# A hybrid decoder block in float32: a list scheduler in the kernel fixes the order of each engine's instructions

## The chip, the cores and the metric

One core of one Trainium2 chip. The metric is device microseconds of one execution of the whole block; lower is better. The kernel before takes 1054.05 us (median of 3 runs, 1053.57 to 1054.77). The engines of the core are called PE (matmuls; PEld is its loading of weights), DVE (VectorE), ACT (ScalarE), POOL (GpSimd) and SP (the queue that issues all the transfers here). Each takes its own instructions strictly in the order in which the compiled program has them, and an instruction that waits holds back all those behind it on its engine.

## The reference

One block over 1024 tokens of width 1024, all float32. A vector c gives shift, scale and gate columns; the rest is two sub-layers with residuals and a last norm:

```python
cond = silu(c) @ ada_w + ada_b
shift1, scale1, gate1, shift2, scale2, gate2 = split(cond, 6)
h = rmsnorm(x, norm1_g) * (1 + scale1) + shift1
u, v, val, gate = split(h @ w_in + b_in, 4)          # 512 columns each
y_a = spatial_gating_mixer(gelu(u), gelu(v), ...)    # layernorm of v, causal 128x128 mix in chunks of 128 tokens
y_b = conformer_conv_mixer(val, gate, ...)           # val * sigmoid(gate), causal depthwise conv of width 31, group norm, silu
y = concat(rmsnorm(y_a), rmsnorm(y_b))
x = x + gate1 * (y @ w_out)
h2 = rmsnorm(x, norm2_g) * (1 + scale2) + shift2
g_ff, up_ff = split(h2 @ w_ffn_in, 2)                # 2 x 2816 columns
x = x + gate2 * ((silu(g_ff) * up_ff) @ w_ffn_out)
out = rmsnorm(x, norm_f_g) * (1 + scale_f) + shift_f
```

## The kernel before, in words

Everything is kept transposed: 128 features on the partitions, tokens along the free dimension, in two halves of 512 tokens. A float32 matmul is made of three fast ones: weights and activations are split into a high part (an ACT copy in the reduced type) and a low part (a subtraction on DVE or POOL), and `mm3` (lines 185 to 189) and `product` (505 to 511) run high x high, low x high and high x low.

**First phase (before about 75 us).** The conditioning columns are dot products: `ada_cols` (133 to 144) loads a 128x1024 tile and DVE multiplies it by silu(c) and sums along the rows (line 143). For each of eight slices of h the shift and the scale column are made, then the slice (`modulated`, 197 to 213), and PE accumulates it into eight PSUM banks of the projections val and gate.

**Mixers.** `u_proj`, `v_proj`, `vg_proj` are the projections of each half of the tokens; `conv_pair` is the convolution, tap by tap on DVE (line 448), for the first half partly on ACT and POOL; `spatial` is the causal mix; `branch_out` the norms; `w_out` the projection back, with the residual into `xs`. During the up-projection x itself lies in HBM (`x_mid`) and its SBUF tiles serve as buffers.

**FFN.** The up-projection uses a 2x2 fast product with seven multiplications over halves of tokens and pairs of tiles: `stationary` (591 to 623) loads the weights of a tile, forms their sums and differences (lines 611 to 617) and splits them (`split`, 501 to 503); `run` accumulates the seven products, and lines 729 to 755 combine them. For 20 of the 22 tiles two of the products, which need the first half of the tokens alone, are made before, while the second half is still in the mixers (`ahead_quad`, 518 to 528, its matmuls at line 510 with the output ah), and put away in HBM. The results go to HBM (line 662) and come back for the down-projection in three rounds, of the same form, which adds into `xs` at line 859. The last 24 conditioning columns (gate2, shift_f, scale_f) are loaded into two tiles of x that are free meanwhile (`last_columns`, 683 to 685, queued by lines 687 to 689) and multiplied by line 143. The last norm and the outputs (lines 807 to 829) close the kernel.

**Buffers.** Tiles with the same tag share a fixed number of slots: three PSUM banks for the tag mm, two each for cv and gn, one for nrm; four slots for raw weights (raw), eight for split ones (w), and so on. A new tile waits for a slot to come free. The pool `ffn` uses the memory of the pools `mid` and `front` again, once these are closed.

**The order.** The framework traces the program, finds the dependences through tiles, and then its own scheduler, which simulates a time line with durations of its own, sets each engine's order: by the program's order as priority, with some work raised (`tc.high_priority`, around the norms) or held back by hand. Four such holds exist, each `with tc.issue_after(ins)`, which lets an engine take what stands in the block only after `ins` on the same engine: the matmuls of `vg_proj(1, (3,), r2_ready, 12)` from the thirteenth slice on (its last 12 matmuls) behind the last matmul of the norm `n2_0` (lines 326 to 328); the loads of the second half of x, of the u weights and of the mixer's operands behind the load of the first phase's last column (line 532); the change of the ACT's table behind the last silu (line 762); and the tail behind an instruction of the down-projection (line 900).

Of the kernel before, what the change touches and what calls it, by code (L numbers as in the profile page):

```python
# [1 line left out]

# [11 lines left out]
P = 128  # L14
# [38 lines left out]
def tile_order():  # L53

    n = N_AHEAD + N_FILL
    whole = {round(i * (NF - 1) / (NF - n - 1)): n + i for i in range(NF - n)}
    begun = iter(range(n))
    return [whole[i] if i in whole else next(begun) for i in range(NF)]


@with_exitstack
def block_kernel(ctx: ExitStack, tc: tile.TileContext, xT, c, ada, cols, vbias, bs, wsp,
                 wv, wu, wvg, wo, wf, wfo, wfl, cst, out):
    nc = tc.nc
    V, A, G, PE = nc.vector, nc.scalar, nc.gpsimd, nc.tensor

    const = ctx.enter_context(tc.tile_pool(name="const", bufs=1))
    sb = ctx.enter_context(tc.tile_pool(name="sb", bufs=1))
# [31 lines left out]
    def hs(half):  # L100
        return slice(half * H, (half + 1) * H)
# [31 lines left out]
    def ada_cols(i, n=1, pool=False, dst=None):  # L133
        for j in range(i, i + n):
            raw = dst
            if raw is None:
                raw = sb.tile([P, D], F32, tag="raw", name=f"ada{j}", bufs=N_RAW)
            ada_dma[j] = nc.sync.dma_start(raw, ada[j])
# [4 lines left out]
            V.scalar_tensor_tensor(raw, raw, 1.0, cact, op0=ALU.mult, op1=ALU.mult,  # L143
                                   accum_out=cond[:, j:j + 1])

    def ccol(m, k, n=1):
        return cond[:, m * 8 + k:m * 8 + k + n]
# [27 lines left out]
    last = {}  # L175
# [139 lines left out]
    first_phase_loaded = ada_dma[SCALE1 * 8 + KD - 1].ins  # L315
# [213 lines left out]


    background += [lambda i=i: ada_cols(GATE1 * 8 + i) for i in range(8)]
    with tc.issue_after(first_phase_loaded):
        for k in range(KD):
            nc.sync.dma_start(xs[k][:, hs(1)], xT[k, :, hs(1)])
        u_proj(0)
        load_mixer_operands()
# [43 lines left out]
    ffn = ctx.enter_context(tc.tile_pool(name="ffn", bufs=1, reuse_waits="tile"))  # L580
# [7 lines left out]
    def ev(name):  # L588
        return ffn.tile([P, H], F32, tag="ev", name=name, bufs=N_EV)
# [35 lines left out]
    for f in range(N_AHEAD, N_AHEAD + N_FILL):  # L625
        t = ffn.tile([P, 2, H], F32, tag="m3", name=f"ahead_{f}", bufs=4)
# [67 lines left out]
    order = tile_order()  # L694
# [118 lines left out]
    def output(i, tiles=range(KD), by_pool=()):  # L813
        bank, part = norm_banks[i], pieces[i]
        size = part.stop - part.start
        if by_pool:
            r = ev(f"r_nf{i}")[:, 0:size]
            A.activation(r, bank[:, 0:size], AF.Copy)
        for k in tiles:
            t = ev(f"of{i}_{k}")[:, 0:size]  # L820
            if k in by_pool:
                G.tensor_tensor(t, xs[k][:, part], r, op=ALU.mult)
                A.activation(t, t, AF.Identity, bias=ccol(SHIFTF, k), scale=ccol(SCALEF, k))
                nc.sync.dma_start(out[k, :, part], t)
                continue
            V.scalar_tensor_tensor(t, xs[k][:, part], ccol(SCALEF, k), bank[:, 0:size],
                                   op0=ALU.mult, op1=ALU.mult)
            A.activation(t, t, AF.Identity, bias=ccol(SHIFTF, k))
            nc.sync.dma_start(out[k, :, part], t)
# [3 lines left out]
    f0 = 0  # L833
    for r, pairs in enumerate(ROUNDS):
        last_round = r == len(ROUNDS) - 1
        mov = [{} for _ in range(pairs)]
        for m in (1, 5, 6, 2, 7, 4, 3):
            for p in range(pairs):
                t = ev(f"a{r}_{p}_{m}")
# [5 lines left out]
        base = 0 if last_round else 8 * r  # L845
# [36 lines left out]
        for n, m in ((0, 1), (0, 5), (0, 6), (0, 2), (0, 7), (1, 1), (0, 4), (0, 3), (1, 6), (1, 2), (1, 7),  # L882
# [4 lines left out]
            last_ins = step(n, m)  # L887
# [29 lines left out]
    output(0, (3, 5, 6, 7), by_pool=(3, 5))  # L917
    output(1)
    output(2)


# [73 lines left out]
```

## Time and profile before

| what | value |
|---|---|
| time, median of 3 runs | 1054.05 us (1053.57 to 1054.77) |
| the profiled execution's own time | 1055.96 us |
| its span, first to last instruction | 1053.9 us |
| granted PE clock, mean over the span | 0.976 |
| PE busy | 983.6 us (93%) |
| DVE busy | 868.5 us (82%) |
| ACT busy | 466.4 us (44%) |
| POOL busy | 413.2 us (39%) |
| moved through HBM | 183 MB, 174 GB/s over the span |

In the profile's lines, times are microseconds from the start of the span. A stretch's row gives its length and, for each engine, the busy time in it with the count of its instructions. A group's row gives line, engine, operation, output<-inputs, shape and count, then the busy time and the mean duration in ns, then the idle time just before these instructions with what ended it. In the chain of work that ended last, each piece stands with its start and duration. "issue" is time in which the engine waited for nothing that the profile shows.

### The profile page before, as it was taken

Reading aid. Unit: us, or ns where it says so; the run is one execution under the profiler, and the core shown is the slowest. Engines: PE = TensorE matmul, PEld = TensorE weight load, DVE = VectorE, ACT = ScalarE, POOL = GpSimd, SP = SyncE. Lnnn points to the kernel's source line nnn. Section 1 sums busy time; section 2 is a strip of 40 time slices with the busy share of each in tenths; the row PEclk is TensorE's granted clock in tenths of the full one; section 3 lists DMA queues with packets and bytes.
Section 4 is the critical chain, followed back from the end, with each engine's and each line's share of the span. In section 5 each row is a group of like instructions: output and inputs, shape, how many; then the busy total and the mean of one; then the engine's idle time right before and its main releaser. Section 6 shows DMA issues by size and latency. Waiting matters only on the chain.

```text
span 1053.9 us, 13171 instructions
## 1 busy us (share of the span) xinstructions
PE 983.6 (93%) x4613; PEld 783.7 (74%) x4613; DVE 868.5 (82%) x1216; ACT 466.4 (44%) x732; POOL 413.2 (39%) x240
## 2 busy tenths in 40 slices
PE   4899999889979999979898999999999999999994
PEld 2677777668757787867686788888887788888873
DVE  5969999689999535399999979879777989968855
ACT  5238575463366444355232233333324725425426
POOL 4509794664625500374044454444444200000041
PEclk9999999999989999989898999999999999999998
DMA  9584351332534543475877646455556955604104
GB/s 337 196 270 158 100 180 60 137 110 97 171 134 159 182 150 130 160 260 200 282 256 252 204 156 219 170 179 195 174 170 227 317 195 188 212 30 155 46 1 159
DMA packets 73567, 183.89 MB, mean 174 GB/s; under 512 B 8188, under 2 KB 10492, under 8 KB 73502
## 3 DMA queue, kind: packets, MB, share of 16 engines
q1 hardware_dynamic: 73502, 183.06, 50.6%
q8 instruction: 36, 0.59, 0.2%
q14 instruction: 29, 0.24, 0.1%
HBM read 141.87 MB, written 41.16 MB: 174 GB/s over the span
## 4 chain that ended last, share of the span: by engine, by line
PE 68%; DVE 19%; DMA 4%; issue 4%; ACT 3%; POOL 1%; SPq 0%; ACTq 0%; DVEq 0%; POOLq 0%
PE B L510 23%; PE C L510 13%; PE ah L510 6%; DVE x L143 3%; PE po L187 3%; PE A L510 3%; PE po L188 3%; PE po L189 3%; DVE w_f L503 2%; PE v L187 2%; PE v L188 1%; PE v L189 1%; PE pu L188 1%; PE p L189 1%; PE pu L189 1%
## 5 line engine op out<-in xcount | busy, mean ns | idle before, releaser
L510 PE MATMUL B<-h,w_f 128*128 128x512 f32 x816 | 199.0, 397 | 9.3 <-DVE w_f L503 4.6
L510 PEld LDWEIGHTS B<-h,w_f 128*128 128x128 f32 x816 | 156.4, 192 | 44.5 <-DVE w_f L503 5.4
L448 DVE SCALAR_TENSOR_TENSOR cv<-ypad,colt,cv 128x512 f32<-128x512 f32 x216 | 149.9, 743 | 0.9
L510 PE MATMUL B<-fa,w_d 128*128 128x512 f32 x528 | 126.8, 390 | 2.8 <-DVE x L859 1.7
L510 PE MATMUL C<-h,w_f 128*128 128x512 f32 x528 | 127.7, 390 | 0.6 <-DVE u L754 0.5
L510 PEld LDWEIGHTS B<-fa,w_d 128*128 128x128 f32 x528 | 98.6, 188 | 25.2 <-DVE x L859 2.5
L510 PE MATMUL ah<-h,wh_a 128*128 128x512 f32 x320 | 106.0, 409 | 11.9 <-DVE ahead L527 6.6
L510 PEld LDWEIGHTS C<-h,w_f 128*128 128x128 f32 x528 | 98.9, 188 | 22.2 <-issue 1.4
L510 PEld LDWEIGHTS ah<-h,wh_a 128*128 128x128 f32 x320 | 62.5, 197 | 28.3 <-DVE ahead L527 7.3
L791 POOL TENSOR_TENSOR sq_nf<-sq_nf,sq_nf 128x512 f32<-128x512 f32 x9 | 12.0, 1345 | 181.9 <-ACT sq_nf L786 181.8
L171 POOL TENSOR_TENSOR wl_a<-raw_a,wh_a 128x1024 fp32r<-128x1024 f32 x20 | 48.7, 2439 | 85.9 <-ACT wh_a L170 84.0
L502 ACT ACTIVATE w_d<-raw_d 128x512 fp32r<-128x512 f32 (+1 forms) x72 | 41.8, 591 | 86.6 <-PE B L510 48.1
L503 DVE TENSOR_TENSOR w_f<-raw_f,w_f 128x512 fp32r<-128x512 f32 x68 | 68.1, 1012 | 5.9 <-ACT w_f L502 5.9
L502 ACT ACTIVATE w_f<-raw_f 128x512 fp32r<-128x512 f32 x68 | 41.6, 625 | 58.6 <-PE B L510 23.9
L752 POOL TENSOR_TENSOR x<-x,up 128x512 f32<-128x512 f32 x20 | 31.6, 1582 | 90.1 <-ACT x L751 90.1
L510 PE MATMUL C<-fa,w_d 128*128 128x512 f32 (+1 forms) x273 | 64.9, 384 | 1.6 <-DVE x L859 1.6
L510 PE MATMUL ah<-h,wl_a 128*128 128x512 f32 x160 | 65.6, 410 | 0.0
L171 POOL TENSOR_TENSOR wl_vg<-raw_vg,wh_vg 128x1024 fp32r<-128x1024 f32 x16 | 44.6, 2793 | 40.5 <-ACT wh_vg L170 40.5
L187 PE MATMUL p<-h,wh_vg 128*128 128x512 f32 x128 | 52.4, 416 | 7.4 <-ACT h L209 6.7
L510 PEld LDWEIGHTS C<-fa,w_d 128*128 128x128 f32 x273 | 50.0, 188 | 12.3 <-DVE x L859 1.8
L189 PE MATMUL p<-h,wh_vg 128*128 128x512 f32 x128 | 49.8, 409 | 3.6 <-DVE h L210 3.6
L503 DVE TENSOR_TENSOR fa<-a,fa 128x512 fp32r<-128x512 f32 x77 | 52.3, 708 | 0.1
(223 smaller groups left out, 2122.5 us busy)
## 6 DMA issues: line engine op xcount, KB each, us to landing
acts<-x SPq DMA_DIRECT2D x77, 256.0 KB, 3.0
a<-acts SPq DMA_DIRECT2D x77, 256.0 KB, 3.7
raw_f<-wf SPq DMA_DIRECT2D x32, 512.0 KB, 4.2
ada<-ada SPq DMA_DIRECT2D x24, 512.0 KB, 3.3
x<-ada SPq DMA_DIRECT2D x24, 512.0 KB, 4.6
raw_a<-wf SPq DMA_DIRECT2D x20, 512.0 KB, 3.3
ahead<-ahead SPq DMA_DIRECT2D x40, 256.0 KB, 2.3
ypad<-ada SPq DMA_DIRECT2D x16, 512.0 KB, 5.0
```

The lines of the kernel that those rows point to most:

```text
L143: V.scalar_tensor_tensor(raw, raw, 1.0, cact, op0=ALU.mult, op1=ALU.mult, accum_out=cond[:, j:j + 1])
L171: lo_eng.tensor_tensor(lo, raw, hi.bitcast(F32), op=ALU.subtract)
L187: PE.matmul(acc, shi, mhi, start=start, stop=False)
L188: PE.matmul(acc, slo, mhi, start=False, stop=False)
L189: PE.matmul(acc, shi, mlo, start=False, stop=stop)
L448: V.scalar_tensor_tensor(accs[j], src, wc, accs[j], op0=ALU.mult, op1=ALU.add)
L502: A.activation(dst[:, 0, :], src, AF.Copy)
L503: lo_eng.tensor_tensor(dst[:, 1, :], src, dst[:, 0, :].bitcast(F32), op=ALU.subtract)
L510: last_mm = PE.matmul(bank[:, cols], s, m[:, cols], start=first and p == 0 and i == 0, stop=p == n - 1 and i == 2, skip_group_check=True)
L752: G.tensor_tensor(g0, g0, up0, op=ALU.mult)
L791: G.tensor_tensor(sums[half], sums[half], t, op=ALU.add)
```

## The change

After everything is traced, and before the framework's scheduler runs, a new function `fix_order` reads the instructions and writes an order for all five queues: each instruction is tied to the one before it on its engine by an edge that is order only (no semaphore). The framework's scheduler then still gives out slots and semaphores, but has no choice left in the order.

- `Step` and `duration` give each instruction its engine, the boxes of the tiles that it reads and writes, the time until its engine can take the next, the time until its result is there, and the time that it holds the port that DVE and POOL share. A matmul of 512 columns is put at 0.2267 us, a transfer at a wait of 2.05 us and 350 GB/s (in) or 1.29 us and 376 GB/s (out).
- `Graph` builds the dependences of data, and the uses of each slot. Tiles of one tag take slots in the program's order, as `Slots` has it; the pool `ffn` gets a slot when the tiles of `mid` and `front` that lie there are done.
- `forward` simulates: of the engines, the one that can start first takes, of its instructions that are ready, the one of the best rank. It doesn't leave an engine idle for something more urgent that comes soon, but for ACT it avoids changes of the function table. `backward` runs the same from the end, and gives each instruction the time from its start to the end.
- `fix_order` goes forward by the program's order, then three times backward and forward, where the rank is the longest time to the end, and keeps the order with the smallest simulated end.

Of the four holds two are gone (the one in `vg_proj` and the one around the loads of the second half of x: both are `nullcontext()` now). The two others become edges of the kernel's own graph, through a local `issue_after`. `tc.high_priority` stays in the code. The computation, the tiles, the slots and the engine of each instruction stay as they are.

```diff
+ENGINES = ("PE", "DVE", "Activation", "Pool", "SP")
+SIGNAL = {"PE": 0.043, "DVE": 0.024, "Activation": 0.024, "Pool": 0.068, "SP": 0.05}
+TABLE_LOAD = 1.295
+LOAD_WAIT, STORE_WAIT, LOAD_RATE, STORE_RATE = 2.05, 1.29, 350e3, 376e3
...
+def duration(s):
+    width = max([o.width for o in s.reads + s.writes] or [0])
+    two_in = sum(o.space == "SB" for o in s.reads) >= 2
+    if s.engine == "PE":
+        n, m = s.writes[0].width, s.reads[1].width
+        if not s.reads[0].f32:
+            t = n / 512 * 0.2267
...
+        if s.kind == "TensorTensor":
+            t, port = 0.138 + width * 0.00106, two_in
...
+class Slots:
+    def blocked_on(self, step):
+        t = 0.0
+        for name in step.slots:
+            tag = self.g.tag_of[name]
+            if name in self.taken:
+                t = max(t, self.taken[name][1])
+            elif self.g.order[tag][self.next[tag]] != name or self.earliest(tag) is None:
+                return tag, t
+            else:
+                t = max(t, self.free[tag][self.earliest(tag)][0])
+        return None, t
...
+class Clock:
+    def run(self, s, t):
+        if s.dma:
+            gap = (TURN_GAP if self.last is False else LOAD_GAP) if s.load else STORE_GAP if self.last else 0.0
+            begin = max(t + (LOAD_WAIT if s.load else STORE_WAIT), self.queue + gap)
+            self.queue = begin + s.bytes / (LOAD_RATE if s.load else STORE_RATE)
+            self.last = s.load
+            self.free["SP"] = t + DMA_ISSUE
+            return t, self.queue
+        if s.port:
+            t = max(t, self.port)
+            self.port = t + s.port
+        self.free[s.engine] = t + s.issue
+        return t, t + s.finish
...
+def forward(g, rank):
...
+    for _ in range(count):
+        t, e = pick(clock, ready, waiting)
+        while waiting[e] and waiting[e][0][0] <= t + 1e-6:
+            n = heapq.heappop(waiting[e])[1]
+            heapq.heappush(ready[e], (rank[n], n))
+        chosen = ready[e][0]
...
+        s = g.steps[chosen[1]]
+        woken = slots.take(s)
...
+        begin, end = clock.run(s, t)
+        done[s.n] = end
+        order[e].append(s)
...
+    return order, done, slots.follows
...
+def fix_order(tc, edges, stacked, reusing, rounds=3):
+    g = Graph(list(tc.nc.cur_bb.bb.instructions), edges, stacked, reusing)
+    order, done, follows = forward(g, list(range(len(g.steps))))
+    best = max(done), order
+    for _ in range(rounds):
+        tail = backward(g, [-t for t in done], follows)
+        order, done, follows = forward(g, [-t for t in tail])
+        best = min(best, (max(done), order), key=lambda b: b[0])
+    for steps in best[1].values():
+        for earlier, later in zip(steps, steps[1:]):
+            tc.add_manual_dep(later.ins, earlier.ins.name,
+                              mybir.DependencyInfo(mybir.DependencyClass.NoSync, mybir.DependencyReason.DATA),
+                              reason="fix_order")
...
+    edges = []
+    @contextmanager
+    def issue_after(ins):
+        n = len(nc.cur_bb.bb.instructions)
+        yield
+        edges.extend((i.name, ins.name) for i in nc.cur_bb.bb.instructions[n:] if i.engine == ins.engine)
...
-                    with tc.issue_after(after) if late else nullcontext():
+                    with nullcontext():
                         mm3(b, unit(w, k), full(h1[half][k]), k == 0, k == KD - 1)
...
-    with tc.issue_after(first_phase_loaded):
+    with nullcontext():
         for k in range(KD):
             nc.sync.dma_start(xs[k][:, hs(1)], xT[k, :, hs(1)])
         u_proj(0)
         load_mixer_operands()
...
-    with tc.issue_after(last["silu"]):
+    with issue_after(last["silu"]):
         A.activation(warm, epst, AF.Sqrt)
...
-    with tc.issue_after(last_ins):
+    with issue_after(last_ins):
         step(1, 3)
...
+    fix_order(tc, edges, ("mid", "front"), "ffn", 3)
```

More of the change, by code (lines that the diff above doesn't have):

```diff
@@ L1 @@
[L1 removed]
+from contextlib import ExitStack, contextmanager, nullcontext
 import concourse.bass as bass
@@ new lines, with operand @@
+class Operand:
+    pass
+def operand(a):
+    o, ap = Operand(), a.bass_ap
+    o.tile, o.name = ap.tensor, ap.tensor.name
+    space = str(ap.tensor.space)
+    o.space = "PSUM" if "PSUM" in space else "DRAM" if "DRAM" in space else "SB"
+    o.width = 1
+    for _, count in ap.ap[1:]:
+        o.width *= count
+    o.f32 = str(ap.dtype).split(".")[-1] == "float32"
+    (pitch, parts), rest = ap.ap[0], ap.ap[1:]
+    p0 = ap.offset // pitch if pitch else 0
+    f0 = ap.offset - p0 * pitch
+    o.box = (p0, p0 + parts, f0, f0 + sum((count - 1) * step for step, count in rest if step > 0) + 1)
+    return o
@@ new lines, in pick, with arrive, wake @@
+def pick(clock, ready, waiting):
+    best = None
+    for e in ENGINES:
+        if ready[e]:
+            t = clock.free[e]
+        elif waiting[e]:
+            t = max(clock.free[e], waiting[e][0][0])
+        else:
+            continue
+        if best is None or t < best[0]:
+            best = t, e
+    t, e = best
+    return t, e
+def forward(g, rank):
+    import heapq
+    count = len(g.steps)
+    need, at = [len(s.before) for s in g.steps], [0.0] * count
+    done, order = [0.0] * count, {e: [] for e in ENGINES}
+    ready, waiting = ({e: [] for e in ENGINES} for _ in range(2))
+    parked = {tag: [] for tag in g.order}
+    slots, clock, table = Slots(g), Clock(), None
+    def arrive(n):
+        tag, t = slots.blocked_on(g.steps[n])
+        if tag is not None:
+            parked[tag].append(n)
+            return
+        heapq.heappush(waiting[g.steps[n].engine], (max(at[n], t), n))
+    def wake(tags):
+        for tag in tags:
+            again, parked[tag] = parked[tag], []
+            for n in again:
+                arrive(n)
+    for s in g.steps:
+        if not need[s.n]:
+            arrive(s.n)
+    for _ in range(count):
[4 more added lines that the diff above has]
+        chosen = ready[e][0]
+        if e == "Activation" and g.steps[chosen[1]].table not in (None, table):
+            others = [x for x in ready[e] if g.steps[x[1]].table in (None, table)]
+            if others and min(others)[0] < chosen[0] + TABLE_LOAD:
+                chosen = min(others)
+        ready[e].remove(chosen)
+        heapq.heapify(ready[e])
+        s = g.steps[chosen[1]]
+        woken = slots.take(s)
+        if s.table not in (None, table):
+            table, t = s.table, t + TABLE_LOAD
+        begin, end = clock.run(s, t)
+        done[s.n] = end
+        order[e].append(s)
+        woken += slots.release(s, end + SIGNAL[e])
+        woken += slots.hand_over() if woken else []
+        wake(woken)
+        for n in s.after:
+            need[n] -= 1
+            same = g.steps[n].engine == e and not s.dma
+            at[n] = max(at[n], (begin + s.issue if e == "PE" else end) if same else end + SIGNAL[e])
+            if not need[n]:
+                arrive(n)
+    return order, done, slots.follows
@@ new lines, in backward @@
+def backward(g, rank, follows):
+    import heapq
+    count = len(g.steps)
+    before = [sorted(s.before) for s in g.steps]
+    need, at, tail = [len(s.after) for s in g.steps], [0.0] * count, [0.0] * count
+    for old, new in follows:
+        for n in g.first[new]:
+            for m in g.final[old]:
+                if m != n:
+                    before[n].append(m)
+                    need[m] += 1
+    ready, waiting = ({e: [] for e in ENGINES} for _ in range(2))
+    clock = Clock()
+    for s in g.steps:
+        if not need[s.n]:
+            heapq.heappush(waiting[s.engine], (0.0, s.n))
+    for _ in range(count):
+        t, e = pick(clock, ready, waiting)
+        while waiting[e] and waiting[e][0][0] <= t + 1e-6:
+            n = heapq.heappop(waiting[e])[1]
+            heapq.heappush(ready[e], (rank[n], n))
+        s = g.steps[heapq.heappop(ready[e])[1]]
+        if s.dma:
+            begin = max(t, clock.queue)
+            clock.queue = begin + s.bytes / (LOAD_RATE if s.load else STORE_RATE) + LOAD_GAP
+            end = clock.queue - LOAD_GAP + (LOAD_WAIT if s.load else STORE_WAIT)
+            clock.free[e] = t + DMA_ISSUE
+        else:
+            begin, end = clock.run(s, t)
+        tail[s.n] = end
+        for n in before[s.n]:
+            need[n] -= 1
+            other = g.steps[n].engine
+            at[n] = max(at[n], begin + s.issue - (s.finish - s.issue) if other == e == "PE" else end + SIGNAL[other])
+            if not need[n]:
+                heapq.heappush(waiting[other], (at[n], n))
+    return tail
```

172 lines of the change are left out of this document (171 added, 1 removed).

## The prediction

> **What bounds the kernel now.** I read the page's head first, then the busy time by stage, then the stages in which TensorE idles, through the chain of work that ended last.
>
> ```profile
> span 1053.9 us, 13171 instructions
> PE 983.6 (93%) x4613; PEld 783.7 (74%) x4613; DVE 868.5 (82%) x1216; ACT 466.4 (44%) x732; POOL 413.2 (39%) x240
> ```
>
> TensorE (PE) is the bound on average, with VectorE (DVE) next. The average hides that the limits differ by stage. Columns of the next view: stretch and its length, busy us and instructions of PE, weight load, DVE, ACT, POOL, then PE's clock, the DMA share and GB/s.
>
> ```profile
> 0.00:20.00 20.00, 8.57 (x45) 3.87 (x45) 8.90 (x16) 13.56 (x20) 4.32 (x10) 1.00 0.87 316
> 20.00:50.00 30.00, 22.64 (x76) 16.95 (x77) 29.59 (x35) 8.08 (x9) 20.10 (x7) 1.00 0.67 246
> 50.00:200.00 150.00, 147.12 (x760) 112.61 (x759) 132.40 (x209) 95.20 (x141) 100.87 (x56) 0.99 0.44 150
> 200.00:235.00 35.00, 28.43 (x206) 22.11 (x205) 28.44 (x36) 16.60 (x22) 20.40 (x11) 0.95 0.36 124
> 300.00:316.00 16.00, 10.65 (x32) 7.49 (x32) 15.96 (x23) 12.44 (x20) 2.75 (x3) 0.69 0.51 174
> 316.00:450.00 134.00, 131.87 (x678) 105.16 (x676) 76.22 (x100) 60.51 (x82) 47.02 (x24) 1.00 0.46 159
> 450.00:600.00 150.00, 133.81 (x545) 107.03 (x544) 146.09 (x191) 54.45 (x92) 63.74 (x38) 0.92 0.71 243
> 600.00:790.00 190.00, 190.00 (x840) 157.34 (x839) 156.40 (x191) 58.75 (x98) 88.24 (x57) 1.00 0.53 182
> 790.00:850.00 60.00, 57.35 (x249) 45.86 (x247) 52.91 (x71) 32.31 (x57) 18.84 (x13) 1.00 0.81 276
> 850.00:1020.00 170.00, 170.00 (x757) 140.40 (x756) 141.52 (x228) 71.21 (x126) 6.88 (x5) 1.00 0.34 115
> ```
>
> Three kinds of stage. From 600 to 790 and from 850 to 1020 PE never idles: 360 us in which an order can save nothing. At 20:50, 300:316 and 450:600 DVE is busy 97 to 100% and PE waits: 7.4, 5.4 and 16.2 us. At 316:450 DVE is idle for 58 us while PE is full, so the DVE work is badly spread, not too much. In 600:790 the rate is that of this piece of the chain, 2.72/12 = 0.227 us for a matmul:
>
> ```profile
> 608.27 2.72 PE B L510 x12
> ```
>
> The waits cost a second time, in clock. These are the six stretches of half clock between start and tail, as they lie in the span (same columns):
>
> ```profile
> 80.00:83.40 3.40, 3.12 (x9) 2.45 (x10) 3.40 (x6) 3.40 (x6) 3.40 (x3) 0.64 0.55 199
> 213.00:216.40 3.40, 1.98 (x8) 1.78 (x8) 2.04 (x3) 3.36 (x5) 2.00 (x1) 0.65 0.04 17
> 305.30:315.50 10.20, 6.35 (x14) 4.57 (x15) 10.20 (x14) 8.32 (x14) 1.66 (x1) 0.54 0.49 155
> 465.70:475.90 10.20, 5.15 (x12) 4.09 (x13) 10.20 (x12) 4.46 (x8) 7.24 (x4) 0.55 0.44 153
> 513.40:520.20 6.80, 4.43 (x10) 3.47 (x11) 6.80 (x12) 1.74 (x2) 0.00 (x0) 0.57 1.01 382
> 561.20:568.00 6.80, 4.14 (x10) 3.29 (x11) 6.80 (x11) 1.15 (x2) 0.91 (x1) 0.57 0.82 264
> sum 40.80, PE 25.18 PEld 19.64 DVE 39.44 ACT 22.42 POOL 15.21; mean PE 4.20 PEld 3.27 DVE 6.57 ACT 3.74 POOL 2.53
> ```
>
> PE works for 25.2 us there at half rate, so 12.6 us are lost beside the idle time itself. All that the middle can lose or give is the idle time of the rows above plus these 12.6 us.
>
> **The change part by part.** No arithmetic is added or removed: same engine, shape and count of compute instructions and transfers; the edges between neighbours on one engine are order only. What moves is the order in each of the five queues. So the sum is of stalls, stage by stage, each as idle + half the PE time at half clock.
>
> *450:600, the largest term*: 16.2 + (5.15 + 4.43 + 4.14)/2 = 23.1 us. The DVE work of this stage, by line:
>
> ```profile
> L143 DVE SCALAR_TENSOR_TENSOR x<-x,cact 128x1024 f32<-128x1024 f32 x24 | 35.4, 1477 | 0.0
> L503 DVE TENSOR_TENSOR w_f<-raw_f,w_f 128x512 fp32r<-128x512 f32 x24 | 21.6, 907 | 0.6 <-ACT w_f L502 0.6
> ```
>
> The 24 products of line 143 are the last conditioning columns; all of them fall here, 35.4 of the 146.1 us. Nothing uses them before the down-projection (about 790). They lie on the chain just ahead of a PE stall:
>
> ```profile
> 511.02 1.15 DVE x L143 x2
> 512.16 0.60 DVE s_f L611
> 512.77 0.43 DVE w_f L503
> ...
> 513.29 0.68 DVE x L616
> 513.97 1.14 DVE x L143 x2
> 515.11 0.61 DVE w_f L503
> ...
> 515.77 10.34 PE B L510 x33
> ```
>
> The new scheduler ranks by the time still to go to the end, so a column needed at 790 ranks behind a weight split needed now. Unhindered, they take 24 x 1.15 = 28 us; DVE idles 190 - 156.4 = 33.6 us in 600:790, so they fit, and 146.1 - 35.4 = 110.7 us are left for 150 (74%). The forward pass never idles DVE on purpose, so some still slip in and hold an urgent split for up to 1.15 us. The other stall is a PSUM bank that DVE drains late, 6.3 us, most of it likewise a matter of rank:
>
> ```profile
> L510 PE MATMUL ah<-h,wh_a 128*128 128x512 f32 x91 | 30.8, 415 | 6.3 <-DVE ahead L527 6.3
> ```
>
> Bounds 0 to 23.1; I take two thirds, 15. What is late next is the weight chain load, subtract, split, which the rest of DVE's work still feeds.
>
> *300:316*: 5.35 + 6.35/2 = 8.5 us. PE waits for h2 tiles while DVE makes them among taps of the convolution:
>
> ```profile
> 300.86 3.38 DVE t_h L199 x5
> 304.24 0.67 DVE cv L448
> ```
>
> DVE has 58 us to spare right after, so taps can go later. Against it: the hold on the last 12 matmuls of the fourth projection pair (until the norm's last matmul) is taken out. Those 12 x 0.227 = 2.7 us fill this hole now; if they run earlier, the hole grows by as much. Bounds -2.7 to 8.5; taken 4.
>
> *200:235*: 6.57 + 1.98/2 = 7.6 us, a latency chain (norms, spatial mix) on DVE that is 81% busy; it can be put in order but not taken out. Bounds 0 to 7.6; taken 4. *50:200*: 2.88 + 3.12/2 = 4.4, taken 2. *316:450*: 2.1, taken 1. *790:850*: 2.65, taken 1; the DMA share of 0.81 speaks against more.
>
> *0:50*: the second hold taken out kept the other half of x behind the first phase's columns:
>
> ```profile
> 32.71 20.53 SPq L138 DMA_DIRECT2D ypad<-ada  x7
> 53.30 4.33 SPq L534 DMA_DIRECT2D x<-xT  x8
> ```
>
> Free of it, the queue may issue those 8 x 256 KB whenever a column waits for its buffer: 2.1 MB at the 316 GB/s of 0:20 is 6.6 us of delay for the columns queued behind, and through them for h1 and PE. On the other side, at most the 7.4 us that PE idles in 20:50. In 20:50 the DMA share is 0.67, so a displaced column has room to catch up, and DVE (29.6 of 30) sets the pace. Bounds -6.6 to 7.4; taken 1.
>
> *Tail*: DVE does four output tiles ahead of the update that the last matmuls wait for:
>
> ```profile
> 1033.67 2.72 DVE of L826 x4
> 1036.39 0.41 DVE x L859
> ...
> 1036.84 1.33 PE C L510 x9
> ```
>
> Up to 2.7 us by rank; the outputs passed over must still be made afterwards, but DVE has room there. Taken 2.
>
> Sum: 15 + 4 + 4 + 2 + 1 + 1 + 1 + 2 = 30 us (upper bound 58.5). The profiled execution took 1055.96 us (span and what lies around it), so 1026; it lies 1.9 us above the median of the runs shown, so I predict 1024.
>
> [...]
>
> **The rivals.**
>
> *Nearly every stall between 50 and 600 goes* (chance 0.22). For: DVE has 58 us free at 316:450 and 33.6 at 600:790, so no stage need be short of it. Against: slots are taken in the program's order for each tag, so work can't move far, and latency chains stay. Time: 23.1 + 8.5 + 7.6 + 4.4 + 2 for the tail = 46, so 1008.
>
> *Stalls are shortened, not removed, and the half clock stays* (0.17). For: the forward pass is greedy, so a column or a tap still lies ahead of urgent work; the planner's clock knows no half rate. Price: a third of the idle time of 50:600 (2.9 + 6.6 + 5.4 + 2.1 + 16.2 = 33 us), 11 + 2 for the tail = 13. Time 1041.
>
> *A fixed transfer queue starves the up-projection* (0.10), the side on which it is slower. One queue (SP) issues all loads and stores. In 600:790 PE is full now, with tiles of 60 matmuls, 13.6 us each, so 14 tiles. If the planner's durations put a store of products ahead of a weight load, and the store waits for POOL, the loads behind it wait too.
>
> ```profile
> SPq L599 <- DVE w_f L503: 73.6, 38, 6.7
> SPq L662 <- POOL x L752: 48.9, 19, 8.7
> ```
>
> Both kinds of wait exist already, up to 8.7 us, hidden by buffers loaded ahead. With 3 us of it bare in each tile it costs 42, less the 30 gained: 1066. It decides from 30/14 = 2.1 us a tile on. Against: PE shows no idle at all there today, and the planner reckons with transfers and buffers.
>
> *The order comes out much as it was* (0.03): the program's order per tag binds so tightly that the queues hardly change; 1054.
>
> **How the numbers follow.** Forecast 0.48 (1024, alone 1014 to 1034), rivals 0.22, 0.17, 0.10, 0.03. The range runs from a little below the first rival (1003) to a little above the second (1049), which leaves out the slower rival and small edges. 0.2% (2.1 us) is about what a measurement can tell from no change. Faster: the forecast and the two faster rivals, less 0.02 for the shallow edge of the second, 0.85; same 0.05; slower 0.10.
>
> **What would show it.** Right: in 450:600 the count of line 143 falls and some stand after 600, PE's idle there is under 6 us with at most one half-clock stretch; 300:316's hole is under 3 us; 600:790 stays at 0.227 us per matmul with PE full. Wrong in 0:50: the second half of x is issued before the last columns and PE starts the steady run later. Wrong in the main: PE idles in 600:790 or 850:1020 behind the transfer queue, or line 143 stays where it is and the stalls go all the same (then rank of drains and splits, not the columns, was the cause).

## The result, and the profile after

The changed kernel takes 1013.09 us (median of 4 runs, 1011.16 to 1013.66), the kernel before, run beside it, 1054.41 us: a ratio of 0.960, with a 95% interval of 0.958 to 0.962. 41 us are gone; 30 were forecast. Lines of the kernel stand 403 further down now: the columns' product of line 143 is line 546, the matmul of line 510 is line 913, the split of line 503 is line 906.

The head of the page after:

```profile
span 1011.4 us, 13149 instructions
PE 967.0 (96%) x4613; PEld 776.3 (77%) x4613; DVE 876.9 (87%) x1216; ACT 466.0 (46%) x727; POOL 421.4 (42%) x240
```

Busy times by stage, in the columns of the prediction (stretch, then PE, weight load, DVE, ACT, POOL, clock, DMA share, GB/s). The work runs ahead of the kernel before by up to some 40 us, so the same stretch holds somewhat later work.

```profile
0.00:50.00 50.00, 27.99 (x100) 18.59 (x101) 37.31 (x48) 21.79 (x29) 21.64 (x16) 0.93 0.91 336
50.00:200.00 150.00, 146.90 (x771) 112.36 (x770) 134.79 (x210) 91.54 (x137) 106.18 (x57) 1.00 0.38 127
200.00:235.00 35.00, 35.00 (x241) 27.71 (x240) 32.27 (x39) 18.08 (x24) 22.88 (x12) 1.00 0.46 151
300.00:316.00 16.00, 16.00 (x71) 12.98 (x70) 16.00 (x25) 10.90 (x18) 12.44 (x7) 1.00 0.70 212
316.00:450.00 134.00, 130.90 (x688) 104.53 (x687) 86.51 (x104) 63.84 (x88) 50.20 (x27) 1.00 0.54 180
450.00:600.00 150.00, 149.35 (x659) 123.33 (x659) 149.25 (x186) 57.90 (x96) 72.43 (x44) 1.00 0.63 210
600.00:790.00 190.00, 189.83 (x838) 156.74 (x836) 177.79 (x228) 72.35 (x120) 89.18 (x56) 1.00 0.71 241
790.00:850.00 60.00, 59.14 (x260) 48.66 (x261) 54.47 (x85) 28.70 (x49) 1.22 (x1) 1.00 0.56 191
```

The holes at 200:235 and 300:316 are closed, and at 450:600 PE idles for 0.65 us instead of 16.2. These are PE's waits in 450:600, with what ended them (total us, times, longest), the three long ones before and the one after:

```profile
PE ah L510 <- DVE ahead L527: 6.3, 1, 6.3
PE B L510 <- DVE w_f L503: 4.6, 2, 3.5
PE B L510 <- DVE x L729: 4.0, 1, 4.0
```

```profile
PE B L913 <- DVE x L1132: 0.7, 1, 0.7
```

Two of the three were PSUM banks that DVE drained late (10.3 us), one was weight splits. What is striking is DVE in that stage: 149.25 of 150 us busy, more than before (146.1), and PE waits for it only once. So a DVE without a free moment is not by itself what stalls PE. Some of its load has also left the stage (the columns, below); the experiments take load and order apart.

The half clock is gone with the holes, but for one stretch in the first phase (same columns) and the start:

```profile
42.00:48.90 6.90, 5.97 (x14) 4.77 (x15) 6.11 (x7) 3.56 (x4) 5.00 (x2) 0.51 0.61 219
```

At the start the clock column misleads: the traces have no record of the clock up to 36.5 us (before) and 31.8 us (after), and the column shows 1.00 there. Up to then the matmuls of 512 columns start 0.43 us apart, as in the half-clock stretches, and 0.23 us apart from then on. So PE ran at half rate in both kernels until then, and the mean clock (0.976 before, 0.990 after) leaves this out.

The columns' product moved, though not all of it: DVE's time on line 546 in two stages (a count of 2 is one column, the product and the read of its sum).

```profile
450.00:600.00 150.00, 12.20 (x20) 1.00 0.63 210
600.00:790.00 190.00, 19.22 (x28) 1.00 0.71 241
```

10 of 24 columns stay in 450:600 and 14 went past 600. The room that they left went to weight splits: 55 subtractions for w_f in the stage instead of 40, for a PE that runs 659 instructions there instead of 545.

The first phase got worse. The transfer queue and the chain of work that ended last, both after:

```profile
12.06 3.28 SPq L937 DMA_DIRECT2D x<-xT  x4
17.57 3.60 SPq L937 DMA_DIRECT2D x<-xT  x4
```

```profile
9.43 6.85 DMA ypad<-ada
16.36 7.75 DMA raw_vg<-wvg
24.18 7.29 DMA ypad<-ada
```

The second half of x is issued from 12 to 21 us, between the first columns; a column or weight tile behind it lands 7 to 8 us after its issue (the median of the 16 loads of columns into ypad is 7.2 us, 5.0 before), and PE has run 100 instructions by 50 us (first row of the stages above), where the kernel before had run 120:

```profile
0.00:50.00 50.00, 31.21 (x120) 20.82 (x121) 38.49 (x50) 21.64 (x29) 24.42 (x16) 1.00 0.75 274
```

### The profile page after: what moved, and what is told of

It is laid out like the page before. It is cut to its first block, busy times and chain, and to the rows that moved or that the text cites. A ratio compares the mean times of both kernels' runs of the same rounds, so it can differ in the third digit from the quotient of the medians.

```text
span 1011.4 us, 13149 instructions
## 1 busy us (share of the span) xinstructions
PE 967.0 (96%) x4613; PEld 776.3 (77%) x4613; DVE 876.9 (87%) x1216; ACT 466.0 (46%) x727; POOL 421.4 (42%) x240
## 4 chain that ended last, share of the span: by engine, by line
PE 82%; DVE 7%; DMA 5%; ACT 3%; issue 2%; POOL 1%; SPq 0%; ACTq 0%; DVEq 0%; POOLq 0%
PE B L913 28%; PE C L913 16%; PE ah L913 10%; PE A L913 3%; PE po L591 3%; PE po L590 3%; PE po L592 3%; PE p L590 2%; PE p L591 2%; PE p L592 2%; PE v L590 2%; PE v L591 1%; PE v L592 1%; DMA ypad<-ada 1%; DVE fa L906 1%
## 5 line engine op out<-in xcount | busy, mean ns | idle before, releaser
L913 PE MATMUL B<-h,w_f 128*128 128x512 f32 x816 | 189.5, 389 | 0.7 <-DVE x L1132 0.7
L913 PEld LDWEIGHTS B<-h,w_f 128*128 128x128 f32 x816 | 153.0, 188 | 32.9 <-DVE x L1132 1.1
L851 DVE SCALAR_TENSOR_TENSOR cv<-ypad,colt,cv 128x512 f32<-128x512 f32 x216 | 147.1, 746 | 0.1
L913 PE MATMUL C<-h,w_f 128*128 128x512 f32 x528 | 123.7, 389 | 0.0
L913 PE MATMUL ah<-h,wh_a 128*128 128x512 f32 x320 | 100.9, 393 | 0.2 <-ACT sg L660 0.2
L1194 POOL TENSOR_TENSOR sq_nf<-sq_nf,sq_nf 128x512 f32<-128x512 f32 x9 | 12.6, 1395 | 184.7 <-ACT sq_nf L1189 184.7
L1155 POOL TENSOR_TENSOR x<-x,up 128x512 f32<-128x512 f32 x20 | 34.9, 1744 | 96.0 <-ACT x L1154 96.0
L913 PEld LDWEIGHTS ah<-h,wh_a 128*128 128x128 f32 x320 | 59.9, 188 | 14.7 <-issue 1.5
L913 PE MATMUL ah<-h,wl_a 128*128 128x512 f32 x160 | 62.7, 394 | 0.0
L590 PE MATMUL p<-h,wh_vg 128*128 128x512 f32 x128 | 53.4, 423 | 9.3 <-ACT h L612 8.6
L1262 DVE SCALAR_TENSOR_TENSOR x<-B,cond,x 128x512 f32<-128x512 f32 x48 | 35.8, 747 | 20.2 <-PE B L913 20.0
```

Of the source, the lines that this page charges most:

```text
L851: V.scalar_tensor_tensor(accs[j], src, wc, accs[j], op0=ALU.mult, op1=ALU.add)
L913: last_mm = PE.matmul(bank[:, cols], s, m[:, cols], start=first and p == 0 and i == 0, stop=p == n - 1 and i == 2, skip_group_check=True)
L1155: G.tensor_tensor(g0, g0, up0, op=ALU.mult)
L1194: G.tensor_tensor(sums[half], sums[half], t, op=ALU.add)
L1262: V.scalar_tensor_tensor(xs[k][:, part], bank[:, cols], ccol(GATE2, k), xs[k][:, part], op0=ALU.mult, op1=ALU.add)
```

## The experiments

Ratios are to the kernel before, run on the same chip.

### The columns, in the kernel before

The first attempt only queues the columns later in the program:

```diff
-    background += [last_columns] * 3
-    background += [lambda i=i: last_columns(2 * i, 2 * i + 1) for i in range(5)]
-    background += [lambda i=i: last_columns(i) for i in range(10, 24)]
+    background += [last_columns] * 9
+    background += [lambda i=i: last_columns(2 * i, 2 * i + 1) for i in range(12)]
```

> The kernel before, with the framework's own order, but the 24 last conditioning columns are queued from the tenth tile of the up-projection on instead of from the fourth. If the columns made the stalls of 450:600 (theory A), PE's idle time there falls from 16.2 us to under 6 and the half-clock stretches at 513 and 561 go: some 12 to 15 us, 1040. If it was the rank of drains and splits as a whole (theory B), at least 11 us of idle stay there and the time is above 1048.

1055.64 us, ratio 1.000 (0.9985 to 1.0013). It tells nothing of the theories, because the columns didn't move: the framework's scheduler still put all 24 before 600. DVE's time on them, in the two stages:

```profile
450.00:600.00 150.00, 34.59 (x48) 0.95 0.75 248
600.00:790.00 190.00, 0.00 (x0) 1.00 0.55 182
```

So the second attempt adds a hold: each column's product comes behind the last update of the tile before.

```diff
         for i in cols:
-            ada_cols(GATE2 * 8 + i, dst=xs[(5, 1)[i % 2]])
+            with tc.issue_after(last["tile"]):
+                ada_cols(GATE2 * 8 + i, dst=xs[(5, 1)[i % 2]])
...
-        V.tensor_tensor(u2, c_bank, u2, op=ALU.add)
+        last["tile"] = V.tensor_tensor(u2, c_bank, u2, op=ALU.add).ins
```

> The kernel before, with DVE's product of each of the 24 last columns held behind an update of the tile before it (two for each tile, from the tenth tile on), so that all of them run after 600. Theory A (the columns overload DVE in 450:600): PE's idle time there falls from 16 us to under 6, the half-clock stretches near 515 and 563 go, and the time is 1038 to 1044. Theory B (the rank of drains and splits as a whole): at least 11 us of idle stay and the time is 1048 or more.

1065.52 us, ratio 1.010 (1.007 to 1.013): slower than before. Busy times by stage, and PE's longest waits over the whole kernel (total, times, longest):

```profile
450.00:600.00 150.00, 140.62 (x608) 115.56 (x607) 130.48 (x152) 57.45 (x96) 70.72 (x43) 0.98 0.51 174
600.00:790.00 190.00, 175.30 (x747) 141.26 (x746) 174.59 (x218) 52.19 (x86) 93.64 (x51) 0.98 0.70 228
```

```profile
PE B L510 <- DVE x L729: 14.7, 10, 2.3
```

Neither theory came out whole: the time is on theory B's side, PE's idle in the stage lies between the two. Without any column DVE is busy for 130 of 150 us in 450:600, and PE still idles for 9.4 us there (16.2 with them). So the columns account for about 7 us of idle, and for some 12 us with the half clock that went along (one stretch of 6.8 us, which costs 2.7, instead of three that cost 8.4). What was won there was lost again in 600:790: two products in every tile, fixed right ahead of the snapshot of bank B (line 729) for which PE waits, cost 0.3 to 2.3 us at ten places, and a stage without idle now has 14.7 us.

### The columns, in the changed kernel

```diff
+            if i == 6:
+                with issue_after(last["column", 0]), issue_after(last["column", 1]):
+                    begin(order[i + 1])
+            else:
+                begin(order[i + 1])
```

(with the columns queued five for each tile, and the two last of them noted in `last`.)

> The changed kernel, with the weights of the eighth tile tied on DVE behind all 24 last columns, so that the new scheduler must put the columns where the kernel before has them. Theory A: PE's stalls come back with them, 8 us or more of idle and half clock in 450:600, and the time is 1021 or more. Theory B: with urgent work ranked first the columns do no harm there; the time is within 4 us of 1013.

1017.73 us, ratio 0.9645 (0.9630 to 0.9659) against 0.9602 (0.9584 to 0.9621) without the tie: 4.6 us lost. The columns' time and all busy times in 450:600:

```profile
450.00:600.00 150.00, 37.03 (x48) 1.00 0.70 239
450.00:600.00 150.00, 142.72 (x616) 114.55 (x615) 148.14 (x194) 48.06 (x84) 68.27 (x41) 1.00 0.70 239
```

All 24 columns stand where the kernel before has them, and PE idles for 7.3 us, at full clock, instead of 16.2 us with 8.4 us lost to half clock beside it. It falls between the two theories. In the changed kernel the place of the columns is worth 4.6 us of the time and 6.6 us of idle in the stage, in the kernel before 7 to 12 us: a fifth to a half of the 24.6 us that the stage lost. The order of everything else is worth more: with all the columns back in the stage and DVE busy for 148 us, 17 of the 24.6 us stay away.

### The hold of the loads

```diff
-    with nullcontext():
+    with issue_after(first_phase_loaded):
         for k in range(KD):
             nc.sync.dma_start(xs[k][:, hs(1)], xT[k, :, hs(1)])
```

> The changed kernel, with the hold of the second half of x and the u weights behind the last column of the first phase put back as edges of the kernel's graph. Theory A: the early loads of x cost the first phase; PE's idle in 0:50 falls from 22.0 us to 18 or less, the half clock at 42:49 goes, and the time falls by 4 to 6 us, to 1008. Theory B: the norm of the second half, which has x early now, gives it back later (a hole at 80 as in the kernel before), and the time stays within 2 us of 1013.

1009.02 us, ratio 0.9565 (0.9545 to 0.9585) against 0.9602 (0.9584 to 0.9621) without the hold: some 4 us better, with intervals that just touch. It is the fastest of all the kernels run. Busy times of the first 50 us:

```profile
0.00:50.00 50.00, 28.14 (x111) 19.25 (x112) 37.52 (x53) 21.80 (x29) 23.29 (x16) 0.97 0.74 267
```

Theory A has the time right, but not all of its detail: PE's idle stays at 21.9 us. PE runs 111 instructions by 50 us instead of 100, because it starts its long run late (at 27.9 us) and then stops only once, for 2.7 us. Half clock is not gone either: one stretch of 3.4 us is left, from 37.1 us on, instead of 6.8. Of the 4 us, 11 x 0.227 = 2.5 us are seen here, the rest lies behind it.

### What the order is made of: rank, port, durations

The changed kernel with the forward pass alone, ranked by the program's order:

```diff
-    fix_order(tc, edges, ("mid", "front"), "ffn", 3)
+    fix_order(tc, edges, ("mid", "front"), "ffn", 0)
```

> The changed kernel with the one forward pass by the program's order as rank, without the passes backward. Theory A: the rank by time to the end makes the gain; half of the stalls of 50:600 come back, the time is 1030 or more. Theory B: a simulation with durations measured by form is enough with any sensible rank; the time is 1013 to 1020.

1038.99 us, ratio 0.984 (0.982 to 0.9855): theory A. 26 of the 41 us go with the passes backward. Its stages:

```profile
50.00:200.00 150.00, 142.15 (x735) 109.23 (x736) 126.69 (x210) 88.33 (x131) 97.47 (x54) 0.97 0.35 117
316.00:450.00 134.00, 126.82 (x659) 100.97 (x658) 84.04 (x110) 60.02 (x82) 43.90 (x23) 0.96 0.49 164
450.00:600.00 150.00, 147.71 (x648) 121.27 (x647) 147.84 (x179) 58.88 (x98) 74.44 (x45) 1.00 0.66 223
790.00:850.00 60.00, 55.04 (x222) 44.14 (x223) 51.23 (x73) 27.05 (x48) 7.75 (x5) 0.91 0.65 227
```

450:600 is almost whole (2.3 us idle) by the program's order as rank; the loss is in the mixers and at the change to the down-projection. The rank by time to the end is worth its 26 us elsewhere than where I looked for them. (These 26 us are the rank and the choice of the best of four simulated orders together; the two were not tried apart.) Nor is it this rank that sends the columns past 600. DVE's time on them here:

```profile
450.00:600.00 150.00, 19.85 (x26) 1.00 0.66 223
```

13 of 24 stay in the stage and 11 go past it, against 10 and 14 with the rank by time to the end.

Next, the scheduler's clock without the port that it has DVE and POOL share (no trace records a port; what the traces show of the two engines stands in the last section):

```diff
-        if s.port:
-            t = max(t, self.port)
-            self.port = t + s.port
```

> The changed kernel, whose scheduler no longer reckons that DVE and POOL share a port. Theory A (durations as the chip has them make the order): DVE's queue is planned some 10% too short where POOL works, PE waits again in 450:790, and the time is 1023 or more. Theory B (the rank is what counts): 1017 or less.

1072.99 us, ratio 1.018 (1.015 to 1.021). These three lines are worth 60 us; without them the whole scheduler is slower than the framework's. In 450:600, all busy times, the time on the columns, and PE's waits in the stage:

```profile
450.00:600.00 150.00, 127.55 (x523) 101.69 (x522) 142.44 (x177) 53.50 (x88) 62.45 (x36) 0.94 0.72 237
450.00:600.00 150.00, 34.41 (x48) 0.94 0.72 237
```

```profile
PE B L910 <- DVE x L1129: 12.4, 4, 4.3
PE ah L910 <- DVE ahead L927: 6.2, 3, 2.8
```

This is the picture of the kernel before over again: all 24 columns in the stage, and PE waiting up to 4.3 us for DVE to snapshot bank B or to drain the bank ah. A planner that believes each subtraction of two SBUF operands to take 0.68 us, where the mean of the 68 that split raw weights (w_f from raw_f) is 0.93 us here and 0.99 in the changed kernel, sees room on DVE that isn't there, puts the columns into it, and everything urgent behind them comes late. The rank is by time to the end in this kernel too, so it is the durations that decide where the columns stand. The stage holds about half of the 60 us (22.5 us of idle, and some 8 us of half clock); the rest is spread over the others. The two holds are out here as well, so taking them out is not enough for the gain. That the framework's scheduler goes wrong for the same reason is likely by this likeness, but its durations were not tried.

Are right means enough? The same kernel, with DVE's `tensor_tensor` operations on two SBUF inputs put 1.4 times as long and POOL's 1.2 times (the taps and the columns' products are another instruction, `scalar_tensor_tensor`, and keep their durations):

```diff
+            t, port = (0.138 + width * 0.00106) * (1.4 if two_in and width >= 256 else 1.0), two_in
...
+            t = (0.21 + width * 0.00211) * 1.2
```

> As the kernel without the shared port in its scheduler, but DVE's operations with two SBUF inputs of 256 or more columns are put 1.4 times as long and POOL's 1.2 times, about the means that the traces show (0.68 to 0.95 us, 1.29 to 1.55 us). Theory A (DVE's planned load was too low): right means are enough and the time is 1022 or less. Theory B (the moment of each collision counts): PE still waits in 450:600 and the time is 1035 or more.

1057.08 us, ratio 1.004 (1.002 to 1.006): theory B by the time. The means recover some 15 of the 60 us:

```profile
200.00:235.00 35.00, 27.92 (x198) 21.94 (x197) 28.89 (x32) 17.45 (x25) 22.73 (x12) 0.90 0.41 130
450.00:600.00 150.00, 141.57 (x607) 114.12 (x606) 149.81 (x185) 56.11 (x93) 72.42 (x42) 0.99 0.72 235
```

450:600 idles 8.4 us instead of 22.5; 200:235, where POOL and DVE meet in another mix, has its 7 us hole. One factor for all is also wrong where POOL is idle (in the changed kernel, 27 of those 68 subtractions overlap no instruction of POOL, and each takes less than 0.7 us), and the columns' products keep 1.15 us in the plan, where their mean was 1.48 us before; so this doesn't tell apart how much is the moment of each collision and how much the means being off.

Last, the port kept, but one duration for each engine:

```diff
-        t = 0.238 + width * 0.0007 if psum else 0.2 + width * 0.00085
+        t = 0.6 if width > 8 else 0.25
...
-        if width <= 8:
-            t = 0.153
+        t = 0.7 if width > 8 else 0.15
...
-                return 1.148, 1.238, 1.068
+                return 0.62, 0.711, 0.55
...
-            t = 0.21 + width * 0.00211
+            t = 1.3
```

> The changed kernel with the shared port, but with one duration for all of DVE's arithmetic (0.70 us), one for ACT's (0.60 us) and one for POOL's (1.30 us) in place of durations by form. Theory A (the port is what the scheduler had to know): 1022 or less. Theory B (durations by form matter as much): 1035 or more.

1058.96 us, ratio 1.005 (1.003 to 1.006): theory B. Its largest losses lie in the mixers:

```profile
50.00:200.00 150.00, 133.79 (x688) 102.67 (x687) 127.25 (x197) 79.67 (x120) 89.97 (x51) 0.95 0.36 118
450.00:600.00 150.00, 142.78 (x651) 115.33 (x650) 144.14 (x172) 61.37 (x101) 73.49 (x41) 1.00 0.68 225
```

16.2 us of idle in 50:200 (3.1 with durations by form), 7.2 in 450:600.

### Which queues have to be fixed

The same planned order, chained on some engines only; the others go by the framework's scheduler.

```diff
-    for steps in best[1].values():
+    for steps in (best[1][e] for e in ("PE", "DVE")):
```

> The changed kernel with only PE's and DVE's instructions chained; ACT, POOL and the transfer queue go by the framework's scheduler. Theory A: the gain lies in DVE's order, PE's follows from it, and the time is within 6 us of 1013. Theory B: the order of loads and of ACT's splits carries a good part; PE idles in 450:790 behind loads or splits and the time is 1025 or more.

> The changed kernel with PE, DVE, ACT and POOL chained and only the transfer queue left to the framework's scheduler. Against the 1040 us with only PE and DVE chained: if the order of transfers carries the difference (theory A), the time stays at 1030 or more; if that of ACT and POOL does (theory B), it falls to 1020 or less.

> The changed kernel with PE, DVE and ACT chained; POOL and the transfer queue go by the framework's scheduler. PE and DVE alone gave 1040 us, all but the transfers 1016. Theory A (ACT's order carries the difference, as DVE waits for its high parts): 1022 or less. Theory B (POOL's order does, through the port): 1030 or more.

> The changed kernel with PE, DVE and POOL chained; ACT and the transfer queue go by the framework's scheduler. Theory A (ACT's order carries the difference): 1032 or more. Theory B (POOL's order does): 1022 or less.

| chained | us | ratio (95%) |
|---|---|---|
| PE, DVE | 1040.10 | 0.9855 (0.9840 to 0.9870) |
| PE, DVE, POOL | 1038.25 | 0.9837 (0.9816 to 0.9858) |
| PE, DVE, ACT | 1017.71 | 0.9656 (0.9633 to 0.9679) |
| PE, DVE, ACT, POOL | 1016.21 | 0.9628 (0.9603 to 0.9654) |
| all five | 1013.09 | 0.9602 (0.9584 to 0.9621) |

By the times, theory B holds for the first two kernels and theory A for the last two. ACT's order is the difference, in both directions: 21 to 22 us with it fixed or left. POOL's order is worth 2 to 3 us and that of the transfers 3, about as much as the intervals are wide. Leaving ACT free also lets go of its one hold (the table change behind the last silu is an edge of the planner's graph); the table then changes at 1010 us instead of 785, but what follows PE's last matmul takes no longer for it (12.3 against 12.6 us), so the 22 us don't come from this. ACT is busy for only 46% of the span, but it stands in the middle of DVE's chains. One wait, first with PE and DVE alone chained, then with all (total, times, longest):

```profile
ACT x L1146 <- DVE x L1145: 53.7, 20, 4.7
```

```profile
ACT x L1146 <- DVE x L1145: 21.3, 12, 2.7
```

The silu waits for its input in the one queue for 54 us in all, in the other for 21, and what stands behind it on ACT waits along. It is not DVE's subtractions that this holds up much: they wait for the high parts of the weights (w_f) for 5.3 us in all in the one, for 2.2 in the other. PE waits for ACT's own work. With PE, DVE and POOL chained, its longest wait between 280 and 800 us is for ACT's snapshot of bank B (line 1130), and with all five chained it is gone:

```profile
PE B L913 <- ACT u L1130: 4.5, 1, 4.5
```

The rest of the 22 us is spread over many places, some 5 us of PE's idle at 235:316 the largest of them; the way each is lost was not followed.

## Why the prediction was right, and where not

The time (1013.1) lies in the range (1003 to 1049), 11 us from the forecast, between it and the first rival (1008). The sign and the main step held: the stalls between 50 and 600 and their half clock were what an order could save, and the 360 us in which PE never idled stayed as they were. Step by step, idle and half clock together:

| stage | lost before, as predicted | lost before, by the trace | taken as gain | measured gain |
|---|---|---|---|---|
| 0:50 | 18.8 idle | 28.1 | 1 | -4.5 |
| 50:200 | 4.4 | 4.6 | 2 | 1.5 |
| 200:235 | 7.6 | 8.1 | 4 | 8.1 |
| 300:316 | 8.5 | 8.7 | 4 | 8.7 |
| 316:450 | 2.1 | 2.3 | 1 | -0.8 |
| 450:600 | 23.1 | 24.6 | 15 | 23.9 |
| 790:850 | 2.65 | 2.65 | 1 | 1.8 |
| the end | 15.5 idle from 850 on | 15.5 | 2 | 0.8 |

The two columns of losses differ because the prediction's six stretches of half clock begin 0.9 us too early: their clock reads 0.54 to 0.65, and 0.50 at the right places, as here (before):

```profile
306.20:316.44 10.24, 7.29 (x16) 5.29 (x17) 10.24 (x16) 8.34 (x15) 1.21 (x2) 0.50 0.53 171
```

PE works for 30.3 us in the six, not 25.2, so they cost 15.2 us, not 12.6. The first row also counts the half rate at the start; the 20 instructions that are missing at 50 us (20 x 0.227 = 4.5) say the same. Over the whole span PE idles 25.9 us less and loses 13.4 us less to half rate, 39 of the 42.5 us between the two spans. The other 3 are in PE's busy time: it pauses 23 times instead of 46, and the last matmul before a pause takes 0.39 us where one that is followed by another takes 0.227, which makes an estimate of 3.7 us.

That the sum of 30 came within 11 of the 41 us is partly luck: the stages from 50 to 850 gave 43 us where 27 were taken, while the start lost 4.5 where 1 was taken and the end gave 0.8 of 2.

- *450:600, 15 taken.* Mis-sized, and for a partly wrong reason. "The 24 products of line 143 ... lie on the chain just ahead of a PE stall" was a true reading of the chain, but the step from there, that DVE would be left at 74% and the stalls go with the load, failed: DVE is at 99.5% and PE at 99.6%. The experiments give the columns 5 to 12 of the 24.6 us. The other step, a bank "that DVE drains late ... a matter of rank", was the larger: 10.3 of the 16.2 us of idle were two such waits, and 17 of the 24.6 us stay away with all the columns back in the stage. It was not a matter of the rank by time to the end, though, and neither was the move of the columns: the program's order as rank leaves 2.3 us of idle and 13 columns in the stage. Durations with the shared port in them did it; without the port the stage has all 24 columns and 22.5 us of idle under the same rank.
- *200:235 and 300:316, 4 each.* Both went entirely (7.6 and 8.5). Halving a stall because it is "a latency chain" was too careful: PE has other work there now and doesn't idle. That the hold on the last 12 matmuls would be missed did not show.
- *0:50, +1 taken, bounds -6.6 to 7.4.* The mechanism of the lower bound came: the second half of x is issued among the first columns. That "a displaced column has room to catch up" was the step that failed: the DMA share rose to 0.91 of the first 50 us, and there was no room. Putting the hold back gave 4 us.
- *The clock.* The terms let the half clock go with the idle time beside it. Whether a stall that is only shortened would have kept its half clock did not show, since the stalls went altogether: one half-clock stretch of 6.8 us is left between start and tail, where the trace before has six, 41 us together.
- *The rivals.* The first, nearly every stall gone (1008), was the better description of the middle; it missed the loss at the start. The second (stalls only shortened, half clock stays) did not come: of the six stretches none is left. The third (starved transfers) did not come: 600:790 idles 0.17 us, and leaving the transfer queue to the framework costs about 3 us. That "the program's order per tag binds so tightly" was a wrong worry as well.

What the prediction didn't see at all is what the gain depends on. The order of one list scheduler was 41 us better than the framework's, or 19 us worse than it, by three lines on a shared port. The prediction reasoned from the rank, which is worth 26 us, and took the planner's durations as given.

## What to carry to other kernels

Where the engine that sets the pace waits for one that is saturated, ask first what that one does ahead of the urgent work: a stage with DVE at 99.5% fed PE almost without a gap once it drained banks and split weights in the right order, while taking a quarter of its load out of the stage by hand won half of the loss there and gave it back where the load was put. A planned order is only as good as its durations (by form, with the shared port in it) and its rank (by the time left to the end): leaving out any one of the three cost 26 to 60 us here, where the whole gained 41. Fix also the queue of the idle-looking engine in the middle of the chain (ACT, 22 us), and keep a hand-written hold where the planner, which takes whatever is ready, would put a load without haste ahead of one that the start waits for.

## What was not expected of the hardware

How much it costs a plan to leave out the port that the scheduler has DVE and POOL share: 60 us, though the subtraction on DVE that splits raw weights only goes from the planned 0.68 us to a mean of 0.99. The mean hides two kinds (after; in the first row the shortest, the median and the longest in ns):

```profile
L906 DVE TENSOR_TENSOR w_f<-raw_f,w_f x68: 673/680/1787, 452.9 to 756.8; 128x512 fp32r<-128x512 f32 x68
```

```profile
L906 DVE TENSOR_TENSOR w_f<-raw_f,w_f 128x512 fp32r<-128x512 f32 x68 | 67.0, 990 | 1.4 <-ACT w_f L905 1.4
```

43 of the 68 take less than 0.7 us. All of the other 25 overlap an instruction of POOL in time, but so do 16 of the 43: an overlap doesn't always cost.

And a long hole left the clock whole where shorter waits came ahead of half clock. After, PE idles for 2.63 us before 105, and the clock from 101 to 115 is 1.00:

```profile
105.14 1.04 PE L641 MATMUL ssq_n<-rt_n,colt 128*128 128x128 f32 x7 [2.63 <-DVE rt_n L639]
```

```profile
101.00:115.00 14.00, 10.99 (x51) 8.52 (x50) 13.89 (x21) 9.69 (x14) 7.42 (x7) 1.00 0.11 37
```

In the kernel before, three waits that make 1.5 us together, behind forty narrow matmuls, come just ahead of the 3.4 us of half clock that start at 80.9:

```profile
76.51 1.30 PE L232 MATMUL ssq_n<-sq_n,ones 128*32 128x128 f32 x40
78.57 0.47 PE L187 MATMUL pu<-h,wh_u 128*128 128x512 f32 x1 [0.77 <-DVE ypad L259]
79.35 0.51 PE L187 MATMUL pu<-h,wh_u 128*128 128x512 f32 x1 [0.30 <-ACT wh_u L170]
80.28 0.50 PE L188 MATMUL pu<-h,wl_u 128*128 128x512 f32 x1 [0.43 <-POOL wl_u L171]
```

```profile
80.93:84.34 3.41, 3.41 (x10) 2.63 (x9) 3.41 (x6) 3.41 (x7) 3.41 (x3) 0.50 0.64 225
```

So in these two traces the length of a hole alone does not tell whether half clock follows. What tells the two cases apart was not shown.
